# Gate columns moved from the retention chunks into the block products, modulation rows moved ahead, split state in two tiles

## Chip, cores and metric

One core of a Trainium2 chip runs the whole kernel. The metric is the device time of one execution in microseconds (us), the median of three runs. The engines are TensorE (PE in the profile, PEld its weight loads), VectorE (DVE), ScalarE (ACT), GpSimd (POOL) and SyncE (SP, which issues most DMAs). Each of them works through its own instructions in the order in which the program lists them; semaphores hold an instruction until what it needs is there.

## What is computed

A decoder block over 1024 tokens of width 1024: an input projection, two token mixers in parallel (retention and dilated attention), a gated merge and an MLP, with each sub-layer modulated by a conditioning vector. The part that matters here:

```python
mod = jax.nn.silu(c) @ w_ada[l] + b_ada[l]
sh1, sc1, g1, sh2, sc2, g2 = jnp.split(mod, 6, axis=-1)
...
rq, rk, rv, rg = parts[0], parts[1], parts[2], parts[3]
...
def step(state, inp):
    qi, ki, vi = inp
    s = jnp.einsum('bhid,bhjd->bhij', qi, ki) * inner_decay[None]
    o = (jnp.einsum('bhij,bhje->bhie', s, vi)
         + jnp.einsum('bhid,bhde->bhie', qi, state) * q_decay[None, :, :, None])
    state = (state * chunk_decay[None, :, None, None]
             + jnp.einsum('bhjd,bhje->bhde', ki * k_decay[None, :, :, None], vi))
    return state, o
...
ret_out = (jax.nn.silu(rg) * ro) @ w_ret_out
```

`ro` is the normalized retention output; four heads of 512 columns make 16 gate columns of 128 for `rg`. The rows `g1`, `sh2`, `sc2` and `g2` of `mod` are used only after the mixers.

## The kernel before

Every fp32 product is made of three products of split operands (a high half rounded to fp32r and a low half, the remainder): `mm3` issues low x high (L207), high x low (L209) and high x high (L211), so these three lines carry nearly all of TensorE's work. Every operand needs a high half (a ScalarE copy) and a low half (a VectorE subtraction). One such product takes a 128x128 weight tile and 512 columns.

The stages run in this order: first values, more values, 20 "pairs" of projections together with rotary embedding, the rest of the values, 32 retention chunks, attention, output projections, MLP.

**The pairs** (`queries_keys`, class `Blocks`). A pair is two output columns of 128. `PAIRS` orders retention queries and keys ("r"), attention queries ("a"), some merge gates ("g") and keys of the third attention group ("k"). A pair is computed from blocks in seven products in place of eight: seven items `ORDER`, each of 4 x 3 products, with sums of blocks formed by VectorE (`prep`) and results combined by VectorE (`post`, `a_out`, L1184). Weights of pair q+2 are loaded while pair q runs (`a_load`). `rotate` applies cos and sin from the tile `cs` (two rows of 1024 per partition) to the "r" pairs, a step after each item. Results go out to DRAM. `values` then makes the remaining value blocks in ten steps of four parts.

**The chunks** (`chunk`, `s_kt`, `on_T`, `u_final`). For every head h (four) and chunk c (eight), g = 8h + c, TensorE works in this order: two kv products of three (`kv`, the chunk's addition to the state, not for c=7), a part of the gate projection (`rg`, `proj_mm`), the scores of the next chunk (`sT`) and its transposed keys (`kT`), the output `o` (six products with the split state `stateh`, `statel`, three with the split scores `smh`, `sml`), the transposes `oT` of the chunk before, and the rest of the `rg` part. One gate column is 48 products and is spread over two chunks, four k blocks (24 products) in each.

Around it, in program order: VectorE updates `state` (L725, or a copy L723 for c=0); a split of the next gate weight (L197 on ScalarE, L198 on VectorE, every second chunk) and one modulation row (L464 to L466, `mod_prep`: a multiply by silu(c) with a sum, then the bias) follow; then `s_kt(g+1)` makes `sm`, its halves `smh`, `sml`, and the key halves `kh`, `kl`. After the products of `o`, ScalarE writes `stateh` and VectorE `statel` (L742, L743) into the one pair of tiles; `jit_qk(g+2)` splits the queries and keys two chunks ahead into `j` (L616 on ScalarE, L617 on GpSimd). The normalization of `o` follows: `bn` statistics, `gr` with a power on GpSimd (L755), `onm`. `u_final` of the head before (c=0 to 3 of the next head) scales and shifts on ScalarE (L687), multiplies by the gate `srg` (L689) and stores y on SyncE's queue. `fetch` loads queries, keys and values three chunks ahead on the same queue.

PSUM has two double banks for `rg` and four single banks for all of `sT`, `kT`, `kv` (twice), `o` and `oT`; a bank is given out again in the order in which it came free.

The stage list gives each chunk its loads, which `Steps` fetches through a ring of three raw tiles:

Of the kernel before, what the change touches and what calls it, by code (L numbers as in the profile page):

```python
# [17 lines left out]
P = 128  # L18
D = 1024
S = 1024  # L20
# [120 lines left out]
def block_kernel(ctx, tc, io, stop=None, dbg=None):  # L141
# [3 lines left out]
    def fv(t):  # L145
        return t.bitcast(F32)
# [19 lines left out]
    def ps_mm(name):  # L166
        return PS["p"].tile([P, 2, 512], F32, tag="mm", bufs=2, name=name)
# [436 lines left out]
    def flat(ps):  # L604
        return ps.rearrange("p a b -> p (a b)")
# [24 lines left out]
    def s_kt(i):  # L630

        p = R["p"]
        g = i
        h, c = divmod(g, NC)
        t = hd["j", g]
        ps = ps_s(f"sT{h}{c}")
        for i in range(2):
            nc.tensor.matmul(ps[:, :2 * C], t[:, 0, 2 + i, :], t[:, :, i, :], start=i == 0, stop=False,
                             skip_group_check=True)
# [12 lines left out]
        nc.scalar.copy(sm, ps[:, :C])  # L652
        nc.vector.tensor_add(sm, sm, ps[:, C:2 * C])
        nc.vector.tensor_mul(sm, sm, decay[:, h * C:(h + 1) * C])
        nc.scalar.copy(smh, sm)
        nc.vector.tensor_sub(sml, sm, fv(smh))
        hd["s", g] = (smh, sml)
        if pk is not None:
            kd = ct[:, CS_KDEC + h:CS_KDEC + h + 1]
            if g == 0:  # L660
                kh, kl = R["kh"], R["kl"]
            else:
                kh = p.tile([P, 2, P], F32R, tag="kh", bufs=1, name=f"kh{h}{c}")
                kl = p.tile([P, 2, P], F32R, tag="kl", bufs=1, name=f"kl{h}{c}")
            nc.scalar.mul(kh, pk, kd)
            nc.vector.scalar_tensor_tensor(flat(kl), flat(pk), kd, fv(flat(kh)), op0=ALU.mult, op1=ALU.subtract)
            hd["k", g] = (kh, kl)

    def on_T(h, c):

# [9 lines left out]
    def u_final(h, es=range(4), queue=nc.sync):  # L680
        for e in es:
# [7 lines left out]
            nc.vector.tensor_mul(t, t, hd["srg", h, e])  # L689
            queue.dma_start(y_d[h][:, 2 * (i % 2):2 * (i % 2) + 2, e // 2], t.rearrange("p (t x) -> p t x", t=2))  # L690

    def chunk(h, c, ahead, w=None):
        p = R["p"]
        g = NC * h + c
        if g + 3 < NG:
            fetch(g + 3)
        if c % 2 == 0:
            hd["rgw"] = w
            hd["rgp"] = ps_mm(f"rg{h}{c}")

        ks = {0: (5, 6, 6), 1: (6, 7, 8)}.get(g) or [4 * (c % 2) + i for i in (0, 2, 4)]
        if g == 0:
            proj_mm(hd["rgp"], hd["rgw"], range(2))
            s_kt(0)
            proj_mm(hd["rgp"], hd["rgw"], range(2, 5))
        vh, vl = hd["v", g][:, 0], hd["v", g][:, 1]
        st, sh, sl = R["state"], R["sh"], R["sl"]
        kvs = []
        if c < NC - 1:
            kh, kl = hd["k", g]  # L710
# [3 lines left out]
                kvs.append(kv)  # L714
        if g == 0:
            s_kt(1)
        proj_mm(hd["rgp"], hd["rgw"], range(*ks[:2]))
        for i, kv in enumerate(kvs):
            if g == 0:
                nc.scalar.copy(sh[:, i, :], kv)  # L720
                nc.vector.tensor_sub(sl[:, i, :], kv, fv(sh[:, i, :]))
            elif c == 0:
                nc.vector.tensor_copy(st[:, i, :], kv)  # L723
            else:
                nc.vector.scalar_tensor_tensor(st[:, i, :], st[:, i, :], float(GAMMA[h] ** C), kv,  # L725
                                               op0=ALU.mult, op1=ALU.add)
        if g == 0:
            jit_qk(2)
        ahead(2)
# [7 lines left out]
        mm3([po], hd["s", g], [(vh, vl)], c == 0, True)  # L737
        for i in range(2) if g == 0 else ():
            nc.scalar.copy(st[:, i, :], kvs[i])
        if g > 0 and c < NC - 1:  # L740
            for i in range(2):
                nc.scalar.copy(sh[:, i, :], st[:, i, :])  # L742
                nc.vector.tensor_sub(sl[:, i, :], st[:, i, :], fv(sh[:, i, :]))  # L743
        if 0 < g < NG - 2:
            jit_qk(g + 2)
        if g > 0:
            on_T(*divmod(g - 1, NC))
        proj_mm(hd["rgp"], hd["rgw"], range(*ks[1:]))
        bn = p.tile([P, 6], F32, tag="bn", bufs=2, name=f"bn{h}{c}")
        ba = p.tile([P, 2], F32, tag="ba", bufs=2, name=f"ba{h}{c}")  # L750
        gr = p.tile([P, 1], F32, tag="gr", bufs=2, name=f"gr{h}{c}")
# [5 lines left out]
        on = p.tile([P, DV], F32, tag="on", bufs=1, name=f"onm{h}{c}")  # L757
        nc.vector.tensor_scalar(on, po, ba[:, 0:1], gr, op0=ALU.subtract, op1=ALU.mult)
        hd["o", h, c] = on
        if c % 2 == 1:  # L760
            hd["srg", h, c // 2] = etile(f"srg{h}{c // 2}")
            nc.scalar.activation(hd["srg", h, c // 2], flat(hd["rgp"]), AF.Silu)
        if h > 0 and c < 4:
            u_final(h - 1, (c,))

# [4 lines left out]
    va_d = [dram.tile([S, 512], F32, name=f"vad{g}") for g in range(3)]  # L770
    aq_d = {(p, g, a): dram.tile([P, S], F32, name=f"aqd{p}{g}{a}") for p in range(2) for g in range(3) for a in range(2)}
    ak_d = {(p, a): dram.tile([P, S], F32, name=f"akd{p}{a}") for p in range(2) for a in range(2)}
    h12_d = [dram.tile([P, 2, 512], F32, name=f"h12d{m}") for m in range(4)]
    xn, wa = [], []

# [359 lines left out]
    a_pairs = [("a", g, p) for p in range(2) for g in range(3)]  # L1135
    g_pairs = [("g", i) for i in range(len(GATES) // 2)]
    k_pairs = [("k", 2, p) for p in range(2)]
    PAIRS = [{"r": r_pairs, "a": a_pairs, "g": g_pairs, "k": k_pairs}[i].pop(0) for i in "rargrarkrargrarkgaga"]
    NA = len(PAIRS)
    OA = {}  # L1140

    def a_load(q, part):
        pair = PAIRS[q]
        src = io[{"g": "w_gate2", "a": "w_aq", "k": "w_ak2"}.get(pair[0]) or f"w_r{pair[1]}"]
        i = 2 * pair[1] + pair[2] if pair[0] == "a" else pair[-1]
        if q == 0 or q % 2 == 0 and part == 2:
            r = x4(f"wa{q}{part}")
        else:
            r = wraw.tile([P, 1024], F32, tag="raw", name=f"wa{q}{part}")
        nc.sync.dma_start(r, src[2 * i + part - 1])  # L1150
        BA.raw[q, part] = r
# [15 lines left out]
    def a_out(q, n, x, y=None):  # L1167
# [9 lines left out]
        elif pair[0] in "ak" and pair[1] == 2:  # L1177
            o = OA[q][i].rearrange("p (r i) -> p r i", r=8)[:, :, 64 * t:64 * t + 64]
            view = lambda z: z.rearrange("p (i r) -> p r i", r=8)
        f = AF.Sigmoid if pair[0] == "g" else AF.Copy  # L1180
        if y is None:
            nc.scalar.activation(o, view(x), f)
        else:
            (nc.vector.tensor_add if n == "12" else nc.vector.tensor_sub)(o, view(x), view(y))  # L1184
            if pair[0] == "g":
                nc.scalar.activation(o, o, f)
        if n in ("12", "21"):
            if pair[0] == "g":
                dst = gate_d[GATES[2 * pair[1] + i]]
            elif pair[0] == "a":  # L1190
                dst = aq_d[pair[2], pair[1], i]
            elif pair[0] == "k":
                dst = ak_d[pair[2], i]
            else:
                return
            nc.sync.dma_start(dst, OA[q][i])
# [15 lines left out]

    gate_d = [dram.tile([P, S], F32, name=f"gated{i}") for i in range(16)]
    BA = Blocks("qa", XA, ["x"] * 4 + ["wh", "wl"] * 3, lambda kind: True, a_place, a_two, a_temps, a_out)

    def queries_keys(ahead):
        for _ in range(4):
# [10 lines left out]
        def after(q, n):  # L1228
# [9 lines left out]
            if n == ORDER[-1] and PAIRS[q][0] == "r":  # L1238
                while turns:
                    drain(turns.pop())  # L1240
                turns.append(rotate(q))
            if q == NA - 1 and n in ("s1", "s4"):
                v_load(n == "s4")
            if q == NA - 1 and n == "12":
# [94 lines left out]
    def values(ahead):  # L1339
        last = len(VSEQ) - 1  # L1340
        for i, (hp, n) in enumerate(VSEQ):
            if i + 2 <= last:
                v_load(i + 2)
            for p in range(4):
# [14 lines left out]
                if p == 2 and i < last:  # L1359
                    v_low(i + 1, 1)  # L1360

                if i == last - 2 and p == 2:
                    fetch(0)
                if i == last - 2 and p == 3:
# [11 lines left out]
        chunk_tiles()  # L1376
        for g in (1, 2):
            fetch(g)
        R["sl"] = R["p"].tile([P, 2, DV], F32R, name="statel")
        R["sh"] = R["p"].tile([P, 2, DV], F32R, name="stateh")  # L1380
        R["state"] = R["p"].tile([P, 2, DV], F32, name="state")
        banks(False)

# [1 line left out]
    steps.add(more_values, manual=True)  # L1385
    steps.add(queries_keys, manual=True)

    later_mods = [G1 + k for k in range(NK)] + [SH2 + k for k in range(NK)] + \
                 [SC2 + k for k in range(NK)] + [G2 + k for k in range(NK)]

    for h in range(H):
        for c in range(NC):
            steps.add((lambda h, c: lambda ahead, *w: chunk(h, c, ahead, *w))(h, c),
                      ([wsplit(io["w_rg"][4 * h + c // 2])] if c % 2 == 0 else []) +
                      [mod_load(later_mods[8 * h + i]) for i in ({0: (0, 1), 1: ()}.get(8 * h + c, (c,)))],
                      manual=True)


# [1423 lines left out]
def pack(x, c, w_ada, b_ada, norm1_g, w_in, rel_bias, ret_gn_g, ret_gn_b,  # L2822
# [14 lines left out]
        "w_rq": _pairs(w[:, 0:1024]),  # L2837
        "w_rk": _pairs(w[:, 1024:2048]),
        "w_rv": _vblocks(w[:, 2048:4096]),
        "w_rg": _cols(w[:, 4096:6144]),  # L2840
# [33 lines left out]
```

## Time and profile before

| | |
|---|---|
| median of three runs | 2175.74 us (2175.16 to 2175.82) |
| the profiled execution, its own time | 2175.49 us |
| span of its instructions | 2173.6 us |
| granted TensorE clock, mean | 0.998 |
| TensorE busy | 2149.8 us |
| VectorE, ScalarE, GpSimd busy | 1512.4, 947.8, 167.3 us |

In the rows of instructions the first number is the start in us from the start of the span, the second the duration in us, then engine, line, operation, and output <- inputs with their shapes; "x2" are two such instructions in a row, and "[0.66 <-POOL gr L755]" says how long the engine stood idle before and what it waited for. TensorE's products are pipelined, so their rows overlap: the distance between two starts, not the duration, is what a product costs. In the rows by stretch, each engine has its busy time in the stretch and the number of its instructions; the last three numbers are the granted TensorE clock, the busy share of the DMA engines and GB/s.

### The profile page before, as it was taken

How to read it: one execution, taken by the hardware profiler on the slowest of the kernel's cores; microseconds unless marked ns; L12 is line 12 of the kernel's file. 1: busy time of each engine (PE TensorE's matmuls, PEld its weight loads, DVE VectorE, ACT ScalarE, POOL GpSimd, SP SyncE). 2: the span in 40 equal slices, each digit the busy share in tenths (PEclk: the TensorE clock that was granted, in tenths of full speed). 3: DMA queues.
4: the chain of work that ended last, by engine and by line, in shares of the span. 5: the costliest groups of instructions: out<-in, count | busy, mean ns of one | idle time of the engine just before them, and what ended most of it. 6: DMA issues, size and time to landing. Idle time of an engine off the chain costs nothing. (4 is left out here: it accounts for less than half of the span.)

```text
span 2173.6 us, 27358 instructions
## 1 busy us (share of the span) xinstructions
PE 2149.8 (99%) x10060; PEld 1788.6 (82%) x10060; DVE 1512.4 (70%) x2361; ACT 947.8 (44%) x1741; POOL 167.3 (8%) x199
## 2 busy tenths in 40 slices
PE   8999999999999999999999999999999999999998
PEld 6888888888887888888888888888778888888887
DVE  5985777776346787786667644677876665977855
ACT  5553322323343445446657625434454455533413
POOL 0001111100002212111110000001000000000003
PEclk9999999999999999999999999999999999999999
DMA  9859998853568565546877365654144435645322
GB/s 382 287 211 301 291 303 229 247 146 116 181 237 304 160 204 189 182 155 195 209 191 206 111 249 208 219 190 134 64 175 160 150 137 196 249 136 174 108 88 78
DMA packets 161522, 420.98 MB, mean 194 GB/s; under 512 B 27877, under 2 KB 55788, under 8 KB 158316
## 3 DMA queue, kind: packets, MB, share of 16 engines
q1 hardware_dynamic: 149112, 370.70, 48.3%
q0 software_dynamic: 9584, 48.24, 10.2%
q8 instruction: 79, 1.29, 0.2%
q10 hardware_dynamic: 2692, 0.30, 0.1%
q14 instruction: 55, 0.45, 0.1%
HBM read 322.03 MB, written 158.23 MB: 221 GB/s over the span
## 5 line engine op out<-in xcount | busy, mean ns | idle before, releaser
L209 PE MATMUL qap<-hl,qaw 128*128 128x512 f32 x240 | 93.4, 389 | 0.0
L207 PE MATMUL qap<-hh,qaw 128*128 128x512 f32 x240 | 93.4, 389 | 0.0
L211 PE MATMUL qap<-hh,qaw 128*128 128x512 f32 x240 | 93.4, 389 | 0.0
L617 POOL TENSOR_TENSOR j<-qk,j 128x512 fp32r<-128x512 f32 x32 | 43.2, 1349 | 441.3 <-ACT j L616 441.3
L2193 POOL TENSOR_TENSOR accnf<-accnf,sqnf 128x256 f32<-128x256 f32 (+1 forms) x18 | 16.6, 921 | 609.6 <-ACT sqnf L2189 609.6
L2297 ACT ACTIVATE a<-a 128x512 f32<-128x512 f32 x48 | 30.3, 631 | 73.1 <-DVE a L2296 73.1
L2505 ACT CAST w2h<-w2s 128x512 fp32r<-128x512 f32 x36 | 22.4, 621 | 79.9 <-DVE w2s L2543 79.9
L264 DVE TENSOR_TENSOR fw<-w1r,fw 128x512 fp32r<-128x512 f32 x48 | 32.9, 688 | 33.5 <-ACT fw L254 33.5
L211 PEld LDWEIGHTS qap<-hh,qaw 128*128 128x128 f32 x240 | 45.1, 188 | 9.4
L209 PEld LDWEIGHTS qap<-hl,qaw 128*128 128x128 f32 x240 | 45.1, 188 | 9.3
L207 PEld LDWEIGHTS qap<-hh,qaw 128*128 128x128 f32 x240 | 45.1, 188 | 9.3
L2028 DVE TENSOR_TENSOR rwl<-rwl,rwh 128x1024 fp32r<-128x1024 f32 x25 | 30.2, 1221 | 29.0 <-ACT rwh L2058 29.0
L207 PE MATMUL fp<-h2h,fw 128*128 128x512 f32 x128 | 50.0, 391 | 0.0
L211 PE MATMUL fp<-h2h,fw 128*128 128x512 f32 x128 | 49.9, 390 | 0.0
L209 PE MATMUL fp<-h2l,fw 128*128 128x512 f32 x128 | 49.8, 389 | 0.0
L652 ACT COPY sm<-sT 128x128 f32<-128x128 f32 x32 | 8.5, 266 | 94.8 <-PE sT L640 94.8
L209 PE MATMUL roa<-rl,rwh 128*128 128x512 f32 x128 | 49.8, 389 | 0.0
L211 PE MATMUL roa<-rh,rwh 128*128 128x512 f32 x128 | 49.8, 389 | 0.0
L207 PE MATMUL roa<-rh,rwl 128*128 128x512 f32 x128 | 49.8, 389 | 0.0
L1561 ACT ACTIVATE P<-P,ng 128x128 f32<-128x128 f32 (+1 forms) x96 | 41.9, 438 | 15.1 <-DVE ng L1553 15.1
L292 DVE TENSOR_TENSOR qat<-qat,qap 128x512 f32<-128x512 f32 x20 | 13.8, 688 | 48.4 <-PE qap L211 48.4
L264 DVE TENSOR_TENSOR qaw<-wa,qaw 128x512 fp32r<-128x512 f32 x60 | 40.0, 686 | 7.1 <-ACT qaw L254 7.1
(3094 smaller groups left out, 7241.7 us busy)
## 6 DMA issues: line engine op xcount, KB each, us to landing
v<-vd SPq DMA_DIRECT2D x32, 512.0 KB, 4.4
raw<-in_w_ada_dram SPq DMA_DIRECT2D x32, 512.0 KB, 5.1
w1r<-in_w_ff_dram SPq DMA_DIRECT2D x32, 512.0 KB, 4.7
yt<-y POOLq DMA_DIRECT2D x24, 512.0 KB, 8.1
xsd<-as SPq DMA_DIRECT2D x24, 512.0 KB, 2.8
w2r<-in_w_ff2s_dram SPq DMA_DIRECT2D x24, 512.0 KB, 6.9
em<-in_w_ada_dram SPq DMA_DIRECT2D x16, 512.0 KB, 10.2
wrvs<-in_w_rv_dram POOLq DMA_DIRECT2D x16, 512.0 KB, 10.6
```

Source lines behind the costliest of these rows:

```text
L207: nc.tensor.matmul(o, wl, xh, start=first, stop=False, skip_group_check=skip)
L209: nc.tensor.matmul(o, wh, xl, start=False, stop=False, skip_group_check=skip)
L211: nc.tensor.matmul(o, wh, xh, start=False, stop=last, skip_group_check=skip)
L264: nc.vector.tensor_sub(t[:, 512:], src, fv(t[:, :512]))
L292: nc.vector.tensor_sub(u, u, b)
L617: nc.gpsimd.tensor_sub(t[:, 1], src, fv(t[:, 0]))
L652: nc.scalar.copy(sm, ps[:, :C])
L1561: nc.scalar.activation(v, v, AF.Exp, bias=ng[:, blk:blk + 1], accum_out=st[:, g, blk, 2 + a:3 + a])
L2028: nc.vector.tensor_sub(lo, fv(lo), fv(hi))
L2193: (nc.vector if f == 7 else nc.gpsimd).tensor_add(G["acc", key], G["acc", key], sq)
L2297: nc.scalar.activation(o, o, AF.Relu)
L2505: nc.scalar.copy(hi, src)
```

## The change

The gate columns of each head are divided. Columns 0 and 1 of each head stay in the chunks; columns 2 and 3 become four "s" pairs at the end of the pairs' stage, are passed through Silu, stored in DRAM (`srg_d`) and loaded in chunks c=4 and 6 of their head. The chunks hold the remaining eight columns at two k blocks a chunk (`RG`; six in the first chunk, one in c=7): one block behind `kv`, the other behind `oT`. The 32 modulation rows are loaded into the tile `cs` from the moment its last rotation is done (`MOD0`), and multiplied, one row every 16/7 items of pairs or parts of values (`mod_turn`), with one bias addition at the end. The split state has two pairs of tiles, so its halves for the next chunk are made right behind the state update, ahead of `s_kt`. In `s_kt`, `kh` and `kl` come ahead of `smh` and `sml`.

```diff
@@ s_kt
-        nc.scalar.copy(smh, sm)
-        nc.vector.tensor_sub(sml, sm, fv(smh))
...
             nc.scalar.mul(kh, pk, kd)
+        nc.scalar.copy(smh, sm)
+        if pk is not None:
             nc.vector.scalar_tensor_tensor(flat(kl), flat(pk), kd, fv(flat(kh)), op0=ALU.mult, op1=ALU.subtract)
             hd["k", g] = (kh, kl)
+        nc.vector.tensor_sub(sml, sm, fv(smh))
@@ new in front of chunk
+    RG = [[2] * (NC - 1) + [1] for _ in range(H)]
+    RG[0][0] = 6
+    def rg_mm(n):
+        for _ in range(n):
+            if hd.get("rgk", NK) == NK:
+                hd["rgk"], hd["rgw"], hd["rgp"] = 0, hd["rgws"].pop(0), ps_mm("rg")
+            proj_mm(hd["rgp"], hd["rgw"], [hd["rgk"]])
+            hd["rgk"] += 1
+            if hd["rgk"] == NK:
+                hd["rgs"] = hd["rgp"]
+    def rg_out(h, c):
+        if "rgs" in hd:
+            i = hd["rgi"] = hd.get("rgi", -1) + 1
+            t = hd["srg", i // 2, i % 2] = etile(f"srg{i // 2}{i % 2}")
+            nc.scalar.activation(t, flat(hd.pop("rgs")), AF.Silu)
+        if c in (4, 6):
+            e = c // 2
+            hd["srg", h, e] = etile(f"srg{h}{e}")
+            nc.sync.dma_start(hd["srg", h, e], srg_d[h, e - 2])
@@ chunk
-        st, sh, sl = R["state"], R["sh"], R["sl"]
+        st, (sh, sl), (sh1, sl1) = R["state"], R["s", (g + 1) % 2], R["s", g % 2]
...
-        proj_mm(hd["rgp"], hd["rgw"], range(*ks[:2]))
+        rg_mm(1 if g == 0 else RG[h][c] - 1)
...
+        if g > 0:
+            for i in range(len(kvs)):
+                nc.scalar.copy(sh1[:, i, :], st[:, i, :])
+                nc.vector.tensor_sub(sl1[:, i, :], st[:, i, :], fv(sh1[:, i, :]))
...
-        if g > 0 and c < NC - 1:
-            for i in range(2):
-                nc.scalar.copy(sh[:, i, :], st[:, i, :])
-                nc.vector.tensor_sub(sl[:, i, :], st[:, i, :], fv(sh[:, i, :]))
...
-        proj_mm(hd["rgp"], hd["rgw"], range(*ks[1:]))
+        rg_mm(0 if g == 0 else 1)
...
-        if c % 2 == 1:
-            hd["srg", h, c // 2] = etile(f"srg{h}{c // 2}")
-            nc.scalar.activation(hd["srg", h, c // 2], flat(hd["rgp"]), AF.Silu)
+        rg_out(h, c)
@@ pairs
-    PAIRS = [{"r": r_pairs, "a": a_pairs, "g": g_pairs, "k": k_pairs}[i].pop(0) for i in "rargrarkrargrarkgaga"]
+    s_pairs = [("s", i) for i in range(H)]
+    PAIRS = [{"r": r_pairs, "a": a_pairs, "g": g_pairs, "k": k_pairs, "s": s_pairs}[i].pop(0)
+             for i in "rargrarkrargrarkgagassss"]
+    MOD0 = 16 * len(ORDER) + 4
@@ new in front of queries_keys
+    NV = 32
+    turn = {"n": 0, "i": 0}
+    def mod_turn():
+        turn["n"] += 1
+        while turn["i"] < NV + 2 and 7 * turn["n"] > 16 * turn["i"]:
+            i = turn["i"]
+            turn["i"] += 1
+            t = cs[:, i % 2]
+            if i > 1:
+                m = G1 + i - 2
+                nc.vector.scalar_tensor_tensor(t, t, 1.0, cb, op0=ALU.mult, op1=ALU.mult, accum_out=mods[:, m:m + 1])
+            if i < NV:
+                nc.sync.dma_start(t, io["w_ada"][G1 + i])
+            if i == NV + 1:
+                m = mods[:, G1:G1 + NV]
+                nc.vector.tensor_add(m, m, vec[:, VC_BADA + G1:VC_BADA + G1 + NV])
@@ queries_keys, after an item; values, after a part
+            if q * len(ORDER) + ORDER.index(n) >= MOD0:
+                mod_turn()
...
+                mod_turn()
@@ values, at its end
-        R["sl"] = R["p"].tile([P, 2, DV], F32R, name="statel")
-        R["sh"] = R["p"].tile([P, 2, DV], F32R, name="stateh")
+        for i in range(2):
+            R["s", i] = [R["p"].tile([P, 2, DV], F32R, name=f"state{n}{i}") for n in "hl"]
@@ loads of the chunks
-                      ([wsplit(io["w_rg"][4 * h + c // 2])] if c % 2 == 0 else []) +
-                      [mod_load(later_mods[8 * h + i]) for i in ({0: (0, 1), 1: ()}.get(8 * h + c, (c,)))],
+                      ([wsplit(io["w_rg"][RGW.index(NC * h + c)])] if NC * h + c in RGW else []),
```

`RGW` lists the chunks in which a gate column begins (0, 2, 6, 10, 14, 19, 23 and 27); its weight is split in the chunk before. The host packs the gate weights accordingly (`w_rg` for the columns that stay, `w_rg2` for the pairs).

More of the change, by code (lines that the diff above doesn't have):

```diff
@@ L696, in chunk @@
             fetch(g + 3)
[L697 to L701, printed above, removed]
+        if w is not None:
+            hd.setdefault("rgws", []).append(w)
         if g == 0:
-            proj_mm(hd["rgp"], hd["rgw"], range(2))
+            rg_mm(2)
             s_kt(0)
-            proj_mm(hd["rgp"], hd["rgw"], range(2, 5))
+            rg_mm(3)
         vh, vl = hd["v", g][:, 0], hd["v", g][:, 1]
-        st, sh, sl = R["state"], R["sh"], R["sl"]
+        st, (sh, sl), (sh1, sl1) = R["state"], R["s", (g + 1) % 2], R["s", g % 2]
         kvs = []
@@ L716, in chunk @@
             s_kt(1)
-        proj_mm(hd["rgp"], hd["rgw"], range(*ks[:2]))
+        rg_mm(1 if g == 0 else RG[h][c] - 1)
         for i, kv in enumerate(kvs):
             if g == 0:
-                nc.scalar.copy(sh[:, i, :], kv)
-                nc.vector.tensor_sub(sl[:, i, :], kv, fv(sh[:, i, :]))
+                nc.scalar.copy(sh1[:, i, :], kv)
+                nc.vector.tensor_sub(sl1[:, i, :], kv, fv(sh1[:, i, :]))
             elif c == 0:
@@ L772, in block_kernel @@
     ak_d = {(p, a): dram.tile([P, S], F32, name=f"akd{p}{a}") for p in range(2) for a in range(2)}
+    srg_d = {(h, i): dram.tile([P, S], F32, name=f"srgd{h}{i}") for h in range(H) for i in range(2)}
     h12_d = [dram.tile([P, 2, 512], F32, name=f"h12d{m}") for m in range(4)]
@@ L1143, in a_load @@
         pair = PAIRS[q]
-        src = io[{"g": "w_gate2", "a": "w_aq", "k": "w_ak2"}.get(pair[0]) or f"w_r{pair[1]}"]
+        src = io[{"g": "w_gate2", "a": "w_aq", "k": "w_ak2", "s": "w_rg2"}.get(pair[0]) or f"w_r{pair[1]}"]
         i = 2 * pair[1] + pair[2] if pair[0] == "a" else pair[-1]
@@ L1179, in a_out @@
             view = lambda z: z.rearrange("p (i r) -> p r i", r=8)
-        f = AF.Sigmoid if pair[0] == "g" else AF.Copy
+        f = {"g": AF.Sigmoid, "s": AF.Silu}.get(pair[0], AF.Copy)
         if y is None:
@@ L1184, in a_out @@
             (nc.vector.tensor_add if n == "12" else nc.vector.tensor_sub)(o, view(x), view(y))
-            if pair[0] == "g":
+            if pair[0] in "gs":
                 nc.scalar.activation(o, o, f)
@@ L1193, in a_out @@
                 dst = ak_d[pair[2], i]
+            elif pair[0] == "s":
+                dst = srg_d[pair[1], i]
             else:
@@ L1386, in block_kernel @@
     steps.add(queries_keys, manual=True)
-    later_mods = [G1 + k for k in range(NK)] + [SH2 + k for k in range(NK)] + \
-                 [SC2 + k for k in range(NK)] + [G2 + k for k in range(NK)]
+    RGW, n = [], 0
+    for g in range(NG):
+        RGW += [g] * (n < 8 * len(RGW) + 1 <= n + RG[g // NC][g % NC])
+        n += RG[g // NC][g % NC]
     for h in range(H):
@@ L2839, in pack @@
         "w_rv": _vblocks(w[:, 2048:4096]),
-        "w_rg": _cols(w[:, 4096:6144]),
+        "w_rg": _cols(w[:, 4096:6144].reshape(1024, 4, 4, P)[:, :, :2].reshape(1024, 1024)),
+        "w_rg2": _pairs(w[:, 4096:6144].reshape(1024, 4, 4, P)[:, :, 2:].reshape(1024, 1024)),
         "w_aq": _pairs(att[:, :, 0].reshape(1024, 1536)),
```

## Prediction

> **What bounds the kernel now.** The page was read first, then the busy time by stage, then the engine rows of one chunk.
>
> ```profile
> span 2173.6 us, 27358 instructions
> PE 2149.8 (99%) x10060; PEld 1788.6 (82%) x10060; DVE 1512.4 (70%) x2361; ACT 947.8 (44%) x1741; POOL 167.3 (8%) x199
> ...
> raw<-in_w_ada_dram SPq DMA_DIRECT2D x32, 512.0 KB, 5.1
> ```
>
> ```profile
> core 0: us, PE busy (x) PEld busy (x) DVE busy (x) ACT busy (x) POOL busy (x), PEclk, DMA share, GB/s
> 0.00:40.00 40.00, 32.80 (x124) 23.97 (x125) 21.24 (x33) 22.69 (x37) 0.20 (x4) 1.00 0.97 372
> 180.00:562.00 382.00, 382.00 (x1687) 316.50 (x1686) 269.44 (x415) 110.12 (x192) 36.23 (x50) 1.00 0.75 225
> ...
> 562.00:670.70 108.70, 107.93 (x477) 89.08 (x475) 52.13 (x65) 46.42 (x68) 7.13 (x10) 1.00 0.70 248
> 670.70:982.60 311.90, 310.60 (x1509) 257.53 (x1509) 244.40 (x513) 143.83 (x361) 57.75 (x62) 1.00 0.55 185
> ```
>
> TensorE is the bound in every stage the change touches: the 20 pairs (180 to 562 us) and the values (to 670.7) leave it no or 0.8 us idle, the 32 retention chunks (311.9 us) 1.3. So a product removed is worth its issue time, as long as no other engine takes over. VectorE has two thirds of the pairs' stage, half of the values' and 78% of the chunks'. One ordinary chunk (head 1, c=5) on TensorE, from its first kv product to the next chunk's:
>
> ```profile
> 799.69 0.39 PE L207 MATMUL kv<-v,kl 128*128 128x512 f32 x1
> ...
> 801.05 0.62 PE L207 MATMUL rg<-hh,raw_6146l 128*128 128x512 f32 x2
> 801.50 0.62 PE L209 MATMUL rg<-hl,raw_6146h 128*128 128x512 f32 x2
> ...
> 803.77 0.28 PE L638 MATMUL sT<-j 128*128 128x256 f32 x1
> ...
> 804.33 0.48 PE L207 MATMUL o<-stateh,j 128*128 128x512 f32 x1
> ...
> 806.50 0.60 PE L676 MATMUL oT<-ct,onm 128*128 128x128 f32 x4
> 806.86 0.71 PE L207 MATMUL rg<-hh,raw_6146l 128*128 128x512 f32 x2
> ...
> 809.71 0.39 PE L207 MATMUL kv<-v,kl 128*128 128x512 f32 x1
> ```
>
> Two products start every 0.455 us (801.05, 801.50), so one costs 0.2275 us although its row lasts 0.39. The chunk takes 10.02 us: kv 1.36, rg 2.72, sT and kT 0.56, o 2.17, oT 0.36, rg 2.85.
>
> VectorE in the same chunk, with a u_final multiply of an earlier one:
>
> ```profile
> 761.51 1.22 DVE L689 TENSOR_TENSOR on<-on,srg 128x1024 f32<-128x1024 f32 x1
> 762.64 1.28 DVE L725 SCALAR_TENSOR_TENSOR state<-state,kv 128x512 f32<-128x512 f32 x2
> ```
>
> ```profile
> 803.18 1.22 DVE L198 TENSOR_TENSOR raw_6363l<-raw,raw_6363h 128x1024 fp32r<-128x1024 f32 x1
> 804.31 1.22 DVE L464 SCALAR_TENSOR_TENSOR raw<-raw,cb 128x1024 f32<-128x1024 f32 x1
> ...
> 805.65 0.28 DVE L653 TENSOR_TENSOR sm<-sm,sT 128x128 f32<-128x128 f32 x1
> 805.97 0.29 DVE L654 TENSOR_TENSOR sm<-sm,decay 128x128 f32<-128x128 f32 x1
> 806.62 0.29 DVE L656 TENSOR_TENSOR sml<-sm,smh 128x128 fp32r<-128x128 f32 x1 [0.36 <-ACT smh L655]
> 807.00 0.48 DVE L666 SCALAR_TENSOR_TENSOR kl<-kT,ct,kh 128x256 fp32r<-128x256 f32 x1
> 807.50 1.29 DVE L743 TENSOR_TENSOR statel<-state,stateh 128x512 fp32r<-128x512 f32 x2
> 808.72 0.69 DVE L752 BATCH_NORM_STATS2 bn<-o 128x6 f32<-128x512 f32 x1
> ...
> 810.53 0.16 DVE L756 TENSOR_TENSOR gr<-gr,ct 128x1 f32<-128x1 f32 x1 [0.66 <-POOL gr L755]
> 810.80 0.81 DVE L758 TENSOR_SCALAR onm<-o,ba,gr 128x512 f32<-128x512 f32 x1
> 811.52 1.28 DVE L725 SCALAR_TENSOR_TENSOR state<-state,kv 128x512 f32<-128x512 f32 x2
> 812.72 1.22 DVE L464 SCALAR_TENSOR_TENSOR raw<-raw,cb 128x1024 f32<-128x1024 f32 x1
> ...
> 816.19 1.29 DVE L743 TENSOR_TENSOR statel<-state,stateh 128x512 fp32r<-128x512 f32 x2 [0.23 <-ACT stateh L742]
> ```
>
> It is a tight series: between two starts there is hardly a gap, and 0.66 us goes to waiting for GpSimd's power. In before this has room, because TensorE's 24 gate products give the chunk 10 us.
>
> **The change, part by part.**
>
> Gate products. Chunks lose half of the gate projection: 8 columns x 8 k x 2 halves x 3 = 384 products, 384 x 0.2275 = 87.4 us. The pairs' stage gains four pairs of 7 x 4 x 3 = 84 products, 336 x 0.2275 = 76.4 us (check: 20 pairs, 20 x 84 x 0.2275 = 382 us, the length of that row). On TensorE alone the change is worth -11.0 us.
>
> The new pairs on VectorE. A pair has 7 lower halves, 4 sums and 5 results of 0.69 us, as 512 columns take in the rows above: 11.0 us. The modulation adds 7 turns x 7/16 = 3.1 rows of 1.34 us (804.31 to 805.65: multiply, accumulator read, add): 4.1. That makes 15.1 of 19.1 us, and 24 values turns add 14 us to 52 of 109. I cost it at nothing; the cover is products prepared several items ahead. Each row load is asked for two turns (4.6 items of 2.73 us, 12.5 us) before its use, and takes 5.1 us by the page. ScalarE's 4 Silu per pair and the 512 KB stores and loads go beside 29% and 34 to 70% of busy time, also at nothing; what follows if that cover fails is rival C. SyncE's loads for the pairs pass the new row loads, whose wait is on VectorE at the same place in the program, so they start at most one multiply later. In the chunks the eight gate loads come in place of eight weight loads and behind y stores that wait for L689 already; fetch works three chunks ahead, 0 us.
>
> What stays in the chunk. TensorE: 10.02 - 12 x 0.2275 = 7.29 us. For c=0, which has only three o products:
>
> ```profile
> 750.64 0.39 PE L207 MATMUL kv<-v,kl 128*128 128x512 f32 x1
> ...
> 759.24 0.39 PE L207 MATMUL kv<-v,kl 128*128 128x512 f32 x1
> ```
>
> 8.60 - 2.73 = 5.87. For c=7 (no kv, six gate products instead of twelve) 7.29 - 1.36 - 1.37 = 4.56, and c=6 has no kT, 7.13.
>
> VectorE: bn to the next state 2.80 (808.72 to 811.52), two state updates 1.20, two lower halves 1.22 and 0.23 of waiting for ScalarE, which the new order puts straight behind the update; sm 0.32 twice, kl 0.50, sml 0.38. That is **6.97**. A u_final multiply (c=0 to 3 of heads 1 to 3) adds 1.13: **8.10**. A weight split (once in four chunks, not in two) adds 1.13 and about 0.4 behind ScalarE's upper half: 1.5. The 1.34 of the modulation row is gone.
>
> So VectorE needs more than TensorE in c=0 to c=4 of heads 1 to 3: 4 x 8.10 + 6.97 + one split 1.5 = 40.9 us against 5.87 + 4 x 7.29 = 35.0. **5.9 us** a head is the new wait. It reaches TensorE by the PSUM banks: four for six tiles a chunk, so o has to wait until the state update has read an older kv tile. That wait already stands once in the trace:
>
> ```profile
> PE o L207 <- DVE state L725: 0.2, 1, 0.2
> ```
>
> The split of the next chunk's j, on ScalarE and GpSimd:
>
> ```profile
> 807.89 0.62 ACT L616 CAST j<-qk 128x512 fp32r<-128x512 f32 x1
> ...
> 808.59 1.36 POOL L617 TENSOR_TENSOR j<-qk,j 128x512 fp32r<-128x512 f32 x1 [7.63 <-ACT j L616]
> ```
>
> c=5 to 7 is short of nothing on VectorE (17.8 against 19.0 us), but c=7 now begins with sT, whose j must be split by ScalarE and GpSimd after the last state product of c=6: 0.62 + 1.36 against 9 products and transposes worth 2.4 us. With ScalarE's queue standing behind the late smh, I take 1.0 of 0 to 2.0. Head 0 has no u_final; its splits and its c=7 I estimate at 1.5. Loss: 3 x 6.9 + 1.5 = 22.2, less the 1.3 us that TensorE already stands in the 311.9: 20.9.
>
> Bounds: TensorE may run on for some 1.5 us before a bank is missing (the o products start 4.6 us behind the first kv), so at the least 5.9 - 1.5 a head and no j wait: 13 us. At the most 5.9 + 2.0 and 0.4 for the second split in each of three heads, and 2 for head 0: 27, less 1.3. The second pair of split state tiles removes a wait worth nothing (behind the o products statel waits the 0.23 of its row or nothing) and is no term; it serves to bring the halves forward.
>
> Sum, against the profiled execution's 2175.49 us: -87.4 + 76.4 + 20.9 = +9.9, which gives **2185.4**. That execution is 0.25 under the median 2175.74, so the median may read 0.2 higher; I leave it.
>
> **Rivals.** A, faster: the VectorE series shortens enough to fit. Were both the 0.66 for GpSimd and the 0.23 for ScalarE hidden, 8.10 becomes 7.21, under 7.29, and from there TensorE decides: -11.0 and some 1 us a head at c=0 and c=7, 2168. For it: VectorE loses 1.34 us a chunk. Against it: the power comes behind j on GpSimd (808.59 + 1.36 ends at 809.95, the power's result is used at 810.53), and j starts no earlier after o than before. 8%.
>
> B, no change: the lower bound, 13 - 1.3 - 11.0 = +1, 2176.5; the banks and the order hide most. 14%.
>
> C, much slower: the new pairs or values stop as well. A row load that takes over 12.5 us makes VectorE stand in front of the lower halves the next products need; at 34 rows and 0.3 us each it is 10 us more, 2195. The values' stage moves data at a share of 0.70 already. Against it: 5.1 us landing, and the 20 pairs keep VectorE 71% full, with rotations, and never stopped TensorE. 14%.
>
> D: repeated short stops lower TensorE's granted clock; a tenth less over the 225 us of chunk work is 25 us, 2210. Against it is the first 40 us, 7.2 us of them idle, at a clock of 1.00. 3%. The Trainium skill, "TensorE: Matmul & The Clock Gate", section "A second HAM failure mode: psum-queue depth-cycling", describes just such micro-idles while banks cycle as a cause of re-throttling; its section on oscillation asks for gaps above about 3.4 us, and the first 40 us, with a granted clock of 1.00, agree with the milder of the two.
>
> **Numbers.** My forecast has 61%; its own range is 2178 to 2190 (net loss 13.5 to 25.7). The measurement can tell about 0.2%, 4.4 us. Faster by more is A: 0.08. Within it are B and the bottom edge of the forecast: 0.15. Slower: 0.77. The range that leaves out 2 in 10 is 2176 to 2194.
>
> **What would show it.** Right: the four Silu pairs run with TensorE unbroken at 19.1 us each; the chunk stage takes about 245 us with some 20 of TensorE idle, most in c=1 to 4 of heads 1 to 3, put down to state (o) and kl (kv), and a j wait at each head's end; VectorE is over 90% full with its GpSimd wait. Wrong: a chunk stage under 232 us (A), idle in qap or vc products (C), a granted clock under 0.98 there (D).

## The result and the profile after

| | before | after |
|---|---|---|
| median of 6 runs, us | 2175.78 | 2184.18 (2183.15 to 2185.54) |
| ratio to before, 95% interval | 1 | 1.0038 (1.0028 to 1.0048) |
| profiled execution, us | 2175.49 | 2184.08 |

The changed kernel is slower by 8.4 us, 0.38%. The first lines of its page, span and busy time of the engines:

```profile
span 2182.2 us, 27317 instructions
...
PE 2144.1 (98%) x10012; PEld 1778.4 (81%) x10012; DVE 1535.6 (70%) x2386; ACT 962.3 (44%) x1773; POOL 164.3 (8%) x199
```

The busy time by stage of the same kernel; the three stretches are the 24 pairs, the values and the 32 chunks:

```profile
core 0: us, PE busy (x) PEld busy (x) DVE busy (x) ACT busy (x) POOL busy (x), PEclk, DMA share, GB/s
180.00:638.40 458.40, 458.40 (x2024) 379.57 (x2023) 334.41 (x520) 138.42 (x240) 36.23 (x50) 1.00 0.73 230
638.40:748.75 110.35, 108.44 (x476) 88.75 (x475) 61.91 (x82) 46.59 (x69) 7.13 (x10) 1.00 0.79 294
748.75:991.10 242.35, 228.32 (x1126) 185.41 (x1125) 191.40 (x414) 129.84 (x344) 54.55 (x62) 1.00 0.51 169
```

Against the lengths of before (382.00, 108.70, 311.90) the pairs grow by 76.4, the values by 1.65, and the chunks shrink by 69.55 us: +8.5, which is the span's +8.6. The chunks had 87.4 us of products taken out (311.9 less 87.4 is 224.5), so 17.85 us of that were given back. Where, TensorE's waits in the chunks say (what TensorE wanted to start, what it waited for, us in all, times, longest):

```profile
PE o L207 <- DVE state L747: 9.4, 14, 1.4
PE sT L638 <- POOL j L617: 3.4, 3, 1.5
PE kv L207 <- DVE kl L666: 0.8, 4, 0.2
```

And two of VectorE's waits there:

```profile
DVE gr L778 <- POOL gr L777: 29.9, 31, 1.0
...
DVE sml L668 <- ACT smh L664: 1.5, 4, 0.4
```

TensorE's bound has become VectorE's: 191.40 us busy plus the 29.9 of waiting for GpSimd are 91% of the stage. VectorE's rows between two state updates of head 1, in a chunk with a u_final multiply (start, duration, operation; the wait before it in brackets):

```profile
830.72 1.28 DVE L747 SCALAR_TENSOR_TENSOR state<-state,kv 128x512 f32<-128x512 f32 x2
832.09 1.29 DVE L752 TENSOR_TENSOR statel<-state,stateh 128x512 fp32r<-128x512 f32 x2
833.30 0.28 DVE L653 TENSOR_TENSOR sm<-sm,sT 128x128 f32<-128x128 f32 x1
...
833.82 0.48 DVE L666 SCALAR_TENSOR_TENSOR kl<-kT,ct,kh 128x256 fp32r<-128x256 f32 x1
...
834.48 0.69 DVE L774 BATCH_NORM_STATS2 bn<-o 128x6 f32<-128x512 f32 x1
...
836.66 0.16 DVE L778 TENSOR_TENSOR gr<-gr,ct 128x1 f32<-128x1 f32 x1 [1.03 <-POOL gr L777]
836.93 0.81 DVE L780 TENSOR_SCALAR onm<-o,ba,gr 128x512 f32<-128x512 f32 x1
837.78 1.23 DVE L690 TENSOR_TENSOR on<-on,srg 128x1024 f32<-128x1024 f32 x1
838.92 1.28 DVE L747 SCALAR_TENSOR_TENSOR state<-state,kv 128x512 f32<-128x512 f32 x2
```

838.92 less 830.72 is 8.20 us, in order and with no gap over 0.11 us but the wait for GpSimd; TensorE's work for the chunk is 7.29. TensorE's rows beside it show who pays: the first o product of a chunk starts only when the first of the two state updates (0.68 us each) is done.

```profile
831.46 0.50 PE L207 MATMUL o<-stateh,j 128*128 128x512 f32 x1 [1.29 <-DVE state L747]
839.66 0.51 PE L207 MATMUL o<-stateh,j 128*128 128x512 f32 x1 [0.66 <-DVE state L747]
```

At the ends of heads 0, 1 and 2 the score product of c=7 waits for the split of j:

```profile
807.27 0.39 PE L638 MATMUL sT<-j 128*128 128x256 f32 x1 [0.82 <-POOL j L617]
...
867.80 0.39 PE L638 MATMUL sT<-j 128*128 128x256 f32 x1 [1.11 <-POOL j L617]
...
928.33 0.39 PE L638 MATMUL sT<-j 128*128 128x256 f32 x1 [1.46 <-POOL j L617]
...
987.26 0.39 PE L207 MATMUL o<-stateh,j 128*128 128x512 f32 x1
```

From one to the next are 60.53 us. By TensorE's own work it would be 5.87 + 5 x 7.29 + 7.13 + 4.56 = 54.0, so heads 1 and 2 lose 6.5 us each, the j waits of 1.11 and 1.46 us at their ends included. The last row is the start of c=7 of head 3, which has no score product left: 58.93 us on, a loss of 4.9.

### The profile page after: what moved, and what is told of

It is laid out like the page before. It is cut to its first block, busy times and chain, and to the rows that moved or that the text cites. A ratio compares the mean times of both kernels' runs of the same rounds, so it can differ in the third digit from the quotient of the medians.

```text
span 2182.2 us, 27317 instructions
## 1 busy us (share of the span) xinstructions
PE 2144.1 (98%) x10012; PEld 1778.4 (81%) x10012; DVE 1535.6 (70%) x2386; ACT 962.3 (44%) x1773; POOL 164.3 (8%) x199
## 3 DMA queue, kind: packets, MB, share of 16 engines
q8 instruction: 79, 1.29, 0.2%
## 5 line engine op out<-in xcount | busy, mean ns | idle before, releaser
L207 PE MATMUL qap<-hh,qaw 128*128 128x512 f32 x288 | 112.0, 389 | 0.0
L209 PE MATMUL qap<-hl,qaw 128*128 128x512 f32 x288 | 112.0, 389 | 0.0
L211 PE MATMUL qap<-hh,qaw 128*128 128x512 f32 x288 | 112.0, 389 | 0.0
L751 ACT CAST stateh<-state 128x512 fp32r<-128x512 f32 x54 | 32.9, 622 | 69.8 <-DVE state L747 62.8
L209 PEld LDWEIGHTS qap<-hl,qaw 128*128 128x128 f32 x288 | 54.1, 188 | 11.3
L207 PEld LDWEIGHTS qap<-hh,qaw 128*128 128x128 f32 x288 | 54.1, 188 | 11.2
L211 PEld LDWEIGHTS qap<-hh,qaw 128*128 128x128 f32 x288 | 54.1, 188 | 11.2
L264 DVE TENSOR_TENSOR qaw<-wa,qaw 128x512 fp32r<-128x512 f32 x72 | 48.1, 686 | 11.2 <-ACT qaw L254 11.2
```

What stands on the lines that cost most here:

```text
L207: nc.tensor.matmul(o, wl, xh, start=first, stop=False, skip_group_check=skip)
L209: nc.tensor.matmul(o, wh, xl, start=False, stop=False, skip_group_check=skip)
L211: nc.tensor.matmul(o, wh, xh, start=False, stop=last, skip_group_check=skip)
L264: nc.vector.tensor_sub(t[:, 512:], src, fv(t[:, :512]))
L751: nc.scalar.copy(sh1[:, i, :], st[:, i, :])
```

## The experiments

The theory is that VectorE's in-order series, with the u_final multiply in it, sets the pace of c=0 to 4. Its rivals were that the PSUM banks or the order of the half states do it whatever VectorE has to do, and that the loss lies in the moved modulation rows. The medians (us), their ratios to before, and the length of the chunk stage:

| kernel | median | ratio (95%) | chunks |
|---|---|---|---|
| after | 2184.18 | 1.0038 (1.0028 to 1.0048) | 242.35 |
| e1_no_mul | 2169.87 | 0.9970 (0.9959 to 0.9981) | 228.6 |
| e2_mul_gpsimd | 2173.79 | 0.9991 (0.9981 to 1.0000) | 231.8 |
| e3_late_halves | 2181.28 | 1.0023 (1.0014 to 1.0033) | 239.3 |
| e4_fast_turns | 2188.41, one run | | 242.3 |
| e5_mods_in_chunks | 2222.89 | 1.0216 (1.0201 to 1.0231) | 284.1 |
| e6_two_pairs | 2175.13 | 0.9997 (0.9988 to 1.0006) | 268.5 |
| e7_combined | 2167.49 | 0.9963 (0.9949 to 0.9977) | 226.4 |
| e8_scores_first | 2193.73 | 1.0082 (1.0067 to 1.0097) | 251.6 |

**The multiply left out** (e1_no_mul).

```diff
-            nc.vector.tensor_mul(t, t, hd["srg", h, e])
+            if queue is not nc.sync:
+                nc.vector.tensor_mul(t, t, hd["srg", h, e])
```

> Leaves out the gate multiply of u_final in the chunks (12 multiplies of 1.13 us on VectorE; heads 0 to 2 come out ungated). VectorE theory: c=0 to 3 of heads 1 to 3 fall from 8.10 to 6.97 us, under TensorE's 7.29, so nearly all of the 9.4 us of o waiting for state goes; chunk stage 242.4 to about 229, time about 2171. Rival (four PSUM banks for six tiles a chunk are too few at the shorter chunk, whatever VectorE has to do): o waits as before, time 2184.

14.3 us less than after. Of the 14.8 us by which the profiled execution is shorter, 13.7 are in the chunks (242.35 to 228.6). The values are 1.6 us shorter as well, which this edit doesn't touch: a stop there comes and goes from run to run (see the values below). TensorE's waits in the chunks:

```profile
PE o L207 <- DVE state L748: 0.8, 5, 0.2
PE sT L638 <- POOL j L617: 2.7, 3, 1.1
```

The o waits fall from 9.4 to 0.8 us, though the banks, the tiles and the order are those of after. So the twelve multiplies of 1.2 us on VectorE cost about 14 us of the kernel's time, as much as they last. Head 0, which has no such multiply in after either, hardly waits there: its o waits are two of 0.16 us.

**The multiply on GpSimd** (e2_mul_gpsimd).

```diff
-            nc.vector.tensor_mul(t, t, hd["srg", h, e])
+            (nc.gpsimd if queue is nc.sync else nc.vector).tensor_mul(t, t, hd["srg", h, e])
```

> The same 12 multiplies on GpSimd in place of VectorE (estimate 2.7 us each, twice the 1.35 of the 512-column j). VectorE theory: as without the multiply, about 2171, since GpSimd has 1.9 us of work in a chunk of 7.3. Rival (GpSimd's power, for which VectorE waits 0.66 to 1.03 us a chunk, comes later behind the multiply, and j with it): VectorE's wait grows by 1 us or more in the 12 chunks and the time stays at 2180 to 2190.

10.4 us less than after, and 3.9 more than without the multiply (3.3 of them in the chunks). The rows of VectorE and GpSimd around one such multiply:

```profile
836.39 1.27 DVE L747 SCALAR_TENSOR_TENSOR state<-state,kv 128x512 f32<-128x512 f32 x2
836.58 2.40 POOL L690 TENSOR_TENSOR on<-on,srg 128x1024 f32<-128x1024 f32 x1 [1.22 <-ACT on L688]
837.76 2.37 DVE L752 TENSOR_TENSOR statel<-state,stateh 128x512 fp32r<-128x512 f32 x2
840.05 0.27 DVE L653 TENSOR_TENSOR sm<-sm,sT 128x128 f32<-128x128 f32 x1
```

The state update, whose kv comes from PSUM, runs at its usual 1.27 beside the multiply. The two subtractions behind it read both operands from SBUF and take 2.37 instead of 1.29: GpSimd ends at 838.98, and they end 1.15 later. So it is in all twelve: no state update is longer than usual, and every subtraction that meets a multiply is, three of them by 1.05 to 1.08 us and nine by 0.13 to 0.16. Over the kernel the subtractions took this much without the multiply (e1_no_mul; the groups of instructions: count, us in all, mean ns),

```profile
L753 DVE TENSOR_TENSOR statel<-state,stateh 128x512 fp32r<-128x512 f32 x54 | 34.9, 689 | 2.5
```

and this with it on GpSimd (e2_mul_gpsimd):

```profile
L752 DVE TENSOR_TENSOR statel<-state,stateh 128x512 fp32r<-128x512 f32 x54 | 39.4, 770 | 2.5
```

The 4.5 us more on VectorE go with the 3.3 us more of the chunks; no run tests whether they are all of the cause.

**The half states late, two pairs of tiles kept** (e3_late_halves).

```diff
-        if g > 0:
-            for i in range(len(kvs)):
-                nc.scalar.copy(sh1[:, i, :], st[:, i, :])
-                nc.vector.tensor_sub(sl1[:, i, :], st[:, i, :], fv(sh1[:, i, :]))
...
         for i in range(2) if g == 0 else ():
             nc.scalar.copy(st[:, i, :], kvs[i])
+        if g > 0:
+            for i in range(len(kvs)):
+                nc.scalar.copy(sh1[:, i, :], st[:, i, :])
+                nc.vector.tensor_sub(sl1[:, i, :], st[:, i, :], fv(sh1[:, i, :]))
```

> Both pairs of state tiles stay, but the halves of the new state are made behind the o products and ahead of j, as in the kernel before, not right behind the state update. VectorE theory: the same VectorE work in another order, kl and sml 1.2 us earlier, no wait of 0.23 for ScalarE: 0 to 4 us faster, 2180 to 2184. Rival (the early halves are what lets the shorter chunk work): slower by 1 us a chunk or more, 2200 and above.

2.9 us less than after. Splitting the state straight behind its update is no gain of the change: it costs a little. The o waits stay (9.9 us), the j waits fall from 3.4 to 1.6.

**Modulation turns closer together** (e4_fast_turns), so that they are done before the values begin.

```diff
-        while turn["i"] < NV + 2 and 7 * turn["n"] > 16 * turn["i"]:
+        while turn["i"] < NV + 2 and 7 * turn["n"] > 10 * turn["i"]:
```

> A modulation row every 10/7 items in place of 16/7, so that all 32 are done before the values' stage begins (48 of 52 turns in the pairs). Theory: the values' 1.65 us over before (110.35 against 108.7, waits for vwl and va) come from the turns in that stage: it returns to about 108.7, and the pairs, with VectorE at 17.6 of 19.1 us, stay without a wait; time 2182.5. Rival (they come from the new pairs just ahead, or from memory traffic): the values' stage stays at 110.3 or the pairs begin to wait.

It was slower, 2188.4 in its one run, with the chunks as they were. The values did get short again: from the last pair product to the first gate product are 109.0 us, where after has 111.9 and before 110.0. But the pairs are 6.8 us longer, because they now stop, by TensorE's waits and by VectorE's from 560 us on:

```profile
PE qap L207 <- DVE qat L293: 5.3, 5, 2.0
...
DVE cossin L1254 <- DMA cossin<-in_w_ada_dram: 5.8, 3, 3.7
```

Over the whole stage six rows come late, 9.0 us in all. Three of TensorE's five stops (3.5 us) come within 3 us behind a late row. The other two (1.7 us, at 578.37 and 599.27) have no late row near: there VectorE, which has more to do in these pairs, is simply behind. The row that was 3.7 us late stopped no product.

A row is asked for two turns ahead, which by TensorE's pace is 7.8 us here (2 x 10/7 items of 2.73) and 12.5 in after. VectorE does not keep that pace, since it falls behind and then takes its turns close together: from the issue of a row to its use are 3.5 to 11.3 us here, 4.3 to 16.4 in after. The landings that the traces keep took up to 6.2 us here and up to 9.4 in after.

**Modulation rows back in the chunks** (e5_mods_in_chunks), with the gate products and the order as in after.

```diff
-            if q * len(ORDER) + ORDER.index(n) >= MOD0:
-                mod_turn()
...
-                mod_turn()
...
-                      ([wsplit(io["w_rg"][RGW.index(NC * h + c)])] if NC * h + c in RGW else []),
+                      ([wsplit(io["w_rg"][RGW.index(NC * h + c)])] if NC * h + c in RGW else []) +
+                      [mod_load(later_mods[8 * h + i]) for i in ({0: (0, 1), 1: ()}.get(8 * h + c, (c,)))],
```

> The modulation rows go back into the chunks' loads (one multiply, read and add of 1.34 us a chunk on VectorE), with no turns in pairs and values; the rest as changed. VectorE theory: 8.31 us in an ordinary chunk and 9.4 with a gate multiply, against 7.29 of TensorE, so nearly every chunk is VectorE's: 32 x 1.34 = 43 us more work, 38 to 42 us of it seen; chunk stage 281 to 285, values 1.7 us shorter, time 2220 to 2225. Rival (the chunk is bound by waits between engines, in which a row more is hidden, as it was in the kernel before): under 2195.

2222.9, and chunks of 284.1, 41.8 us more than after for 32 rows of 1.34 = 42.9: with VectorE as the bound, what it is given is paid about in full. Part of the price may be the clock, which was lowered there for 13.6 us (last section). TensorE's waits in the chunks:

```profile
PE o L207 <- DVE state L747: 17.0, 19, 1.4
PE kv L207 <- DVE kl L666: 9.2, 6, 1.6
PE sT L638 <- POOL j L617: 8.9, 3, 3.9
```

**Two Silu pairs instead of four** (e6_two_pairs): 12 of the 16 column blocks stay in the chunks, with three gate steps per chunk.

```diff
-    RG = [[2] * (NC - 1) + [1] for _ in range(H)]
-    RG[0][0] = 6
+    RG = [[3] * (NC - 1) + [2] for _ in range(H)]
+    RG[0][0], RG[3][7] = 6, 3
...
-             for i in "rargrarkrargrarkgagassss"]
+             for i in "rargrarkrargrarkgagass"]
...
-        "w_rg": _cols(w[:, 4096:6144].reshape(1024, 4, 4, P)[:, :, :2].reshape(1024, 1024)),
-        "w_rg2": _pairs(w[:, 4096:6144].reshape(1024, 4, 4, P)[:, :, 2:].reshape(1024, 1024)),
+        "w_rg": _cols(w[:, 4096:6144].reshape(1024, 4, 4, P)[:, :, :3].reshape(1024, 1536)),
+        "w_rg2": _pairs(w[:, 4096:6144].reshape(1024, 4, 4, P)[:, :, 3:].reshape(1024, 512)),
```

> Two Silu pairs in place of four: 12 gate columns stay in the chunks, at three k blocks a chunk (TensorE 8.65 us in an ordinary chunk, VectorE 6.97 to 8.10 as before and a split in every 2.7 chunks). VectorE theory: TensorE decides again nearly everywhere, o waits under 3 us in all; pairs 38.2 us shorter, chunks some 23 longer instead of 43.7; time about 2169, faster than both kernels, though TensorE has 5.5 us more products than in the changed one. Rival (what is lost in the chunks does not hang on how full VectorE is): 2184 + 5.5 = 2190.

No difference from before that can be measured. Its stretches by busy time (pairs, values, chunks):

```profile
180.00:600.20 420.20, 420.20 (x1856) 347.93 (x1855) 306.62 (x476) 124.50 (x216) 36.32 (x50) 1.00 0.75 233
600.20:712.00 111.80, 109.35 (x478) 89.00 (x476) 68.91 (x95) 46.55 (x69) 8.34 (x10) 1.00 0.84 312
712.00:980.50 268.50, 266.17 (x1316) 221.34 (x1317) 197.81 (x418) 141.02 (x352) 54.78 (x62) 1.00 0.49 158
```

The mechanism is as forecast: with 10.02 - 6 x 0.2275 = 8.66 us of TensorE work in a chunk VectorE's 8.2 fits, and the chunks take TensorE's own 311.9 - 192 x 0.2275 = 268.2. The time is a miss of the expectation's arithmetic: it took more off the chunks than the 17.85 us they had lost, and nothing for the values, which take 3.1 us more than in before: with 14 items fewer in the pairs, 38 of the 76 turns fall into them, and not 24. Pairs +38.2, values +3.1 and chunks -43.4 make -2.1; the span is only 1.0 shorter (2172.6 for 2173.6), as the stages ahead of the pairs and behind the chunks took some 1 us more.

**All that helped together** (e7_combined): multiplies on GpSimd, half states late, and in c=7 the one gate step ahead of the score product, so that the split of j has time.

```diff
-            nc.vector.tensor_mul(t, t, hd["srg", h, e])
+            (nc.gpsimd if queue is nc.sync else nc.vector).tensor_mul(t, t, hd["srg", h, e])
...
-        rg_mm(1 if g == 0 else RG[h][c] - 1)
+        rg_mm(1 if g == 0 or c == NC - 1 else RG[h][c] - 1)
...
-        rg_mm(0 if g == 0 else 1)
+        rg_mm(0 if g == 0 or c == NC - 1 else 1)
```

with the move of e3_late_halves.

> The changed kernel with the 12 gate multiplies on GpSimd, the state halves behind the o products, and in c=7 its six gate products ahead of sT, not behind oT, so that j has 1.4 us more. VectorE theory: the three gains add up as far as they lie in different places: 10.4 + 2.9 + up to 3.6 (the sT waits for j), less what they share; 2167 to 2171. Rival (the GpSimd multiply, 2.4 us with statel held behind it, now holds the score products on VectorE instead): no better than 2174.

2167.49: 8.3 us faster than before, 16.7 than after, and the fastest kernel here. Its chunk stage by busy time:

```profile
747.20:973.60 226.40, 224.44 (x1124) 185.69 (x1123) 178.84 (x399) 128.68 (x340) 85.99 (x73) 1.00 0.56 181
```

TensorE's longest wait left there:

```profile
PE o L207 <- DVE state L747: 0.9, 6, 0.2
```

That is 1.9 us over TensorE's 224.5, and the j wait is gone. The chunks are 15.95 us shorter than in after. GpSimd and the late halves alone gave 10.5 and 3.0 of that; the other 2.4 go with the 3.4 us of j waits, though that order was not run by itself. In the profile the values are 1.8 us shorter too, as in e1_no_mul.

**The old order in s_kt** (e8_scores_first), scores ahead of keys.

```diff
+        nc.scalar.copy(smh, sm)
+        nc.vector.tensor_sub(sml, sm, fv(smh))
         hd["s", g] = (smh, sml)
...
-        nc.scalar.copy(smh, sm)
         if pk is not None:
...
-        nc.vector.tensor_sub(sml, sm, fv(smh))
```

> The order in s_kt is put back (smh and sml ahead of kh and kl), the rest as changed. VectorE theory: the series has the same instructions but stands 0.3 to 0.4 us more for ScalarE's smh in each chunk, and kl comes later than the next kv in the full chunks: kv waits of some 9 us, time 2190 to 2195. Rival (the order is worth nothing where VectorE is full anyway): 2184.

9.5 us more than after. By TensorE's waits in the chunks (as listed above for after) the keys come later, and the state with them:

```profile
PE o L207 <- DVE state L747: 12.2, 13, 1.2
PE kv L207 <- DVE kl L667: 6.2, 6, 1.0
PE sT L638 <- POOL j L617: 3.9, 3, 2.2
```

And VectorE waits again between the two halves of the scores:

```profile
DVE sml L656 <- ACT smh L655: 11.7, 32, 0.4
```

The new order puts kl into that gap, which leaves 1.5 us in after. 11.7 less 1.5 is near the 9.5 that the order is worth.

## Why the prediction was right, and where it was off

**Gate products, -87.4 and +76.4.** Right: the pairs grew by 76.4 us with TensorE busy in 458.40 of 458.40.

**The new pairs at nothing.** Right, and its cover was tested: at a lead of 12.5 us no product waits; at 7.8 (e4_fast_turns) rows are late and rival C's mechanism appears.

**The values at nothing.** Mis-sized: they took 1.65 us more. TensorE's stops in them, in after:

```profile
PE va L207 <- ACT va L1378: 1.1, 1, 1.1
PE vc L209 <- DVE vwl L1330: 0.5, 1, 0.5
PE va L209 <- DVE vwlTrue L1332: 0.3, 1, 0.3
```

Without turns in the values (e4_fast_turns, e5_mods_in_chunks) there is no such stop, and from the last pair product to the first gate product are 109.0 us against 111.9. So the stops come with the turns. The largest stands behind a transfer. SyncE asks for the weights `vwlTrue` 3.3 us after the last pair product, in after as in e5_mods_in_chunks; ScalarE has waited for them until 10.3 us after it in after, until 7.9 there. This stop comes and goes: in e1_no_mul and e7_combined, with the same turns, these weights are there at 8.9 and 8.6 us, ScalarE holds no `va`, and the values take 110.4 and 110.1 us. One statement of the prediction failed on the way: that SyncE's other loads start "at most one multiply later". Two loads (`vm`) stood behind a row's load and were issued 4.0 us ahead of the last pair product, against 15.5 in e5_mods_in_chunks. Whether this is what delays the weights was not tested.

**The chunks, 20.9 us lost.** The mechanism was right, the size 3.05 too high (17.85). VectorE's chunk with a multiply was put at 8.10 and took 8.20; inside it two errors met: the wait for GpSimd is 1.03 here, 0.96 in the mean, not 0.66, while of ScalarE's 0.23 a gap of 0.09 is left and the small operations follow each other more closely. A head was put at 6.9 us and lost 6.5, 6.5 and 4.9, which makes 17.9 for 20.7. Its j wait was right, 1.0 against 0.8 to 1.5 at the ends of heads 0 to 2. Too large were the 5.9 us of VectorE: without the j waits, and some 0.2 us of each that lie under the row before, a head lost 5.2, 4.9 and 4.9. The likely reason is that TensorE runs on for a while before it has to stop, which the sum left out and only its lower bound had (1.5 us a head); no run tests it. The 1.5 for head 0 was about right: TensorE's stops there are 0.31, 0.16, 0.21 and 0.16 us and the j wait of 0.82; they take the place of the 1.3 us of before.

The wait appears where it was said to, at o behind state; of the kv waits only 0.8 us came. e1_no_mul shows the cause: without the multiply the loss is 228.6 - 224.5 = 4.1. That the wait passes through the PSUM banks is read from the program, as everything that o itself reads is a chunk old; no run had another number of banks.

**"Some 20 us of TensorE idle."** 242.35 - 228.32 is 14.0. A product's row lasts 0.39 us and the next one starts after 0.2275, so some 0.2 us of each stop lie under the row before it. The loss has to be read from the stage's length.

**The second pair of tiles worth nothing by itself.** This stays open, since one pair of tiles with late halves was not tried. What it serves, the early halves, costs 2.9 us (e3_late_halves).

**A step without a term.** The new order in s_kt went into VectorE's series of 6.97 unspoken, as sml 0.38 with no wait for ScalarE. It is worth 9.5 us (e8_scores_first); without it the change would have come out at 2193.7, above the forecast's own range (2178 to 2190). The forecast rests on it, though no term names it.

**The sum.** -3.05 in the chunks and +1.65 in the values leave +8.5 for +9.9: two errors of opposite sign, and that the second takes off half of the first is luck.

**The rivals.** A needs a stage under 232 us; e1_no_mul and e7_combined show what it takes, the multiply off VectorE. B's 2176.5 lies below the runs (2183.15 at the least). Of C, one sign came in small: a vc product waits 0.5 us; but no row is late and nothing waits in qap. D did not occur, with a granted clock of 1.00 in all three stretches, but the argument against it was not sound: in the first 40 us the view says 1.00, while TensorE's products there (av, 128x512) start every 0.43 us until 15.3 us and every 0.23 from then on, so they began at about half pace. And stops shorter than the 3.4 us of its milder rule are enough (2.5 us in e5_mods_in_chunks, below).

## What to carry to other kernels

When work is taken from the engine that bounds a stage, add up the next engine's in-order series for one loop period, its waits for other engines included, and not only its busy share: at 78% VectorE had room for TensorE's 10.0 us a chunk, and none for 7.3. From there what it does is paid about in full, so order inside a chunk that could be worth at most the 1.3 us for which TensorE stood in before (keys ahead of scores, one operation on another engine) becomes worth as much as the products that were moved (9.5 and 10.4 us against 11.0). And a transfer started some operations ahead is as safe as that distance in us on the engine that uses it, at its shortest: 12.5 us by TensorE's pace held and 7.8 did not, though each landing that the trace of the second keeps took 6.2 or less.

## What the hardware showed beside that

**GpSimd beside VectorE.** The 128x1024 multiply took 2.40 us on GpSimd and 1.22 on VectorE, and VectorE's subtractions with both operands in SBUF waited behind it (2.37 for 1.29, above) while the state update with an operand in PSUM did not. The Trainium skill, "SBUF — State Buffer", section "SBUF: two separate sides", says that the two engines share a port pair which one instruction holds to its end and the other waits for, VectorE among other cases when it reads two inputs from SBUF; the rows agree.

**The clock after longer stops.** In e5_mods_in_chunks the score product of c=7 waited three times, at 813.27 and 884.76 us for 2.5, and at 956.09 for 3.92:

```profile
956.09 0.58 PE L638 MATMUL sT<-j 128*128 128x256 f32 x1 [3.92 <-POOL j L617]
```

The granted clock by stretch of that stage (behind the busy times of the engines):

```profile
806.00:826.00 20.00, 17.41 (x83) 13.71 (x82) 16.71 (x40) 7.82 (x24) 3.60 (x4) 0.91 0.58 193
826.00:886.00 60.00, 48.69 (x229) 37.30 (x228) 49.69 (x106) 29.76 (x78) 12.54 (x14) 1.00 0.63 209
886.00:896.00 10.00, 10.00 (x46) 8.24 (x45) 8.61 (x21) 3.66 (x11) 1.83 (x2) 0.83 0.61 209
896.00:946.00 50.00, 42.65 (x196) 32.29 (x195) 42.58 (x93) 25.25 (x66) 9.97 (x11) 1.00 0.62 204
946.00:966.00 20.00, 16.05 (x70) 12.98 (x69) 14.87 (x33) 8.15 (x21) 4.40 (x6) 0.83 0.66 226
```

It fell to 0.91 and 0.83 in the stretches with those stops or just behind them and was 1.00 between, where shorter stops of TensorE, up to 1.69 us, go on. These are means: in narrower stretches the clock is 0.50 from 814.3 to 817.7, from 886.0 to 889.3 and from 954.3 to 961.0 us, and 1.00 between. In after, stops up to 1.46 us left it at 1.00, and the longest that did so in any profile here is 2.18 us (e8_scores_first, at 935.45). So a lowered clock, which rival D feared from repeated short stops, goes here with single ones of 2.47 us and more, longer than this change makes; the tie is by place in the trace, and was not tested apart.
